# A float32 matmul in place of three split ones: the first expert's gate and up weights, and the first token tile's first projection

## The chip, the cores and the metric

One Trainium2 chip; the kernel uses one of its cores. The metric is the device time of one execution in microseconds (us), as the median of several executions. Engines are named as the profile names them: PE (TensorE matmuls; PEld its weight loads), DVE (VectorE), ACT (ScalarE), POOL (GpSimd), SP (SyncE, whose queue issues most loads).

## The reference, cut to what matters

Two layers over 512 tokens of 1024 features, all in float32: four attention mixers, then a mixture of 16 experts of which each token uses two.

```python
for layer in range(DEPTH):                       # 2
    h = rms_norm(x, norm1_g[layer])
    proj = jnp.einsum('bsd,dc->bsc', h, w_in[layer])
    ...
    x = x + jnp.einsum('bsm,md->bsd', mixed, w_out[layer])
    x = x + hier_moe(rms_norm(x, norm2_g[layer]), ...)

def hier_moe(h, wg, bg, we, be, w_gate, w_up, w_down):
    ...                                          # gate: top group, then top 2 experts of it
    for e in range(N_EXPERTS):                   # 16
        hid = jax.nn.silu(t @ w_gate[e]) * (t @ w_up[e])
        y = y + gate[:, e:e + 1].astype(t.dtype) * (hid @ w_down[e])
```

## The kernel before, in words

**Split operands.** Weights come in units of 128 x 1024 float32 (512 KB; the first projection's are 128 x 832). A unit is loaded into a buffer `raw`, and `split` (L142 to L145) makes of it two tiles in PE's rounded format: ACT copies `raw` to `hi`, and an engine E subtracts, `lo = raw - hi`; E is DVE, or POOL where the table `TAIL` says `sG`. Activations are split the same way (`hTh`/`hTl`, `xh`/`xl`, `hh`/`hl`). A product is then three matmuls, hi x hi, hi x lo, lo x hi (`mm3`, L263 to L269).

**The class `Weights`** keeps the units in order of use. A unit's `raw` is given back as soon as it is split, and the next load is issued on SP then; six units may be split ahead of PE (`HL = 6`).

**The start.** The 512 tokens are four tiles of 128. Tile t's rows are multiplied by the norm weights `g1` into `h` (`gained`, L587 to L593: tile 0 on DVE, tiles 1 to 3 on POOL in layer 0), turned by PE in eight pieces of 128 x 128 (`turned`), split, and multiplied with the first piece of `w_in`, 416 columns in four units (`proj`, L600). The rows' own scale `r0` is a chain of twelve small DVE operations (`rstd`, L124 to L135) and is put on by ACT when the product leaves PSUM (`ca`, L707); the sums of squares for it are ACT's `sq` (L585). ACT's order there is `ca` of tile 0, `sq` of tile 2, `hTh` of tile 2.

**Around the start of the experts.** The attention stage ends with a list of words in `TAIL`, which a small interpreter runs in that order: `x3` gathers expert 0's rows by matmul into `acc` (L1142), and then word list 69, "T K m sG B O q sG S": T turns `acc` into expert 0's `xh` and `xl`, K works out the gates on DVE (L1341 to L1368) and their three bf16 parts (L1334, L1336), m clears a buffer, sG splits a unit with POOL, B stores the last tile, O is a branch for overfull experts, q copies the token numbers, S issues the gather of expert 1's rows on POOL's DMA queue.

Then the loop over `MOE_ORDER` runs: gate and up of expert 0, then for each expert the next gate, this one's down, the next up. Each step splits what is ahead, multiplies one unit (`gu`, L1416; six matmuls of 512 columns) and frees it. Between expert 0's up units PE also runs the row lists `pli` (L1389, four small matmuls each), which need one-hot tiles `oh` from DVE (L341) and K's parts, and the eight transposes `ptg` of expert 1's rows (L1413).

Of the kernel before, what the change touches and what calls it, by code (L numbers as in the profile page):

```python
# [11 lines left out]
FT = mybir.dt.float32  # L12
# [3 lines left out]
AF = mybir.ActivationFunctionType  # L16
OP = mybir.AluOpType
AX = mybir.AxisListType

S = 512  # L20
D = 1024
NT = 4
# [3 lines left out]
CAP = 96  # L26
# [18 lines left out]
        66: "e1 sG c2",  # L45
        67: "f0 b3G o2 p0 r1V f1 h1 d2 o3 r2G e2 x0 p1 c3 d3 f2 e3 h30 x1 r3G p2 h2 f3",
        68: "x2 h31 p3 l x3",
        69: "T K m sG B O q sG S"}
WAITP = 5
JOIN = 52  # L50
STORES = ((13, 0, 1), (6, 1, 2), (1, 2, 3), (0, 3, 4))
# [11 lines left out]
def hybrid_encoder(ctx: ExitStack, tc: tile.TileContext, I: dict, out: bass.AP, depth=2, dbg=None):  # L63
# [10 lines left out]
    x_sb = cst.tile([128, NT, D], FT, name="x_sb")  # L74
# [68 lines left out]
    def split(hi, lo, src, E=V):  # L143
        A.activation(hi, src, AF.Copy)  # L144
        E.tensor_tensor(lo, src, hi.bitcast(FT), op=OP.subtract)  # L145

    class Weights:
# [4 lines left out]
        def __init__(self):  # L152
            self.spec, self.raw, self.hl, self.where = [], {}, {}, {}
            self.loaded = self.done = self.used = 0
            self.moe_pools = []
            self.held, self.paused = 0, False
            self.spare, self.spare_upto = [], 0

        def add(self, src, k, n, moe=False):
            self.spec.append((src, k, n, moe))  # L160
# [2 lines left out]
        def load(self, upto, q=SP, spare=False):  # L163
            while self.loaded < min(upto, len(self.spec)) and not self.paused:
# [22 lines left out]
                self.raw[u] = r  # L187
                self.loaded += 1

        def split(self, upto, E=V):  # L190

            while self.done < min(upto, self.loaded) and self.done < self.used + self.HL - self.held:
                u = self.done
                src, k, n, moe = self.spec[u]
                hi = wp.tile([128, 1024], FR, name="hi", bufs=self.HL)[:, :k * n]
                lo = wp.tile([128, 1024], FR, name="lo", bufs=self.HL)[:, :k * n]
                split(hi, lo, self.raw.pop(u), E)
                r = self.where.pop(u)
                if isinstance(r, bass.AP):
                    self.spare.append(r)  # L200
                self.hl[u] = (hi.rearrange("p (k n) -> p k n", k=k), lo.rearrange("p (k n) -> p k n", k=k))
                self.done += 1
                self.load(len(self.spec))
# [10 lines left out]
        def free(self, upto):  # L214
            for u in range(self.used, upto):
                del self.hl[u]
            self.used = upto

    W = Weights()
# [3 lines left out]
    def add_piece(key, w, c0, n, kc, per, moe=False, parts=1, pairs=False):  # L223

        if pairs:
            wv = w.rearrange("(i p j) n -> p i j n", p=128, j=2)
            us = [W.add(wv[:, k0 // 2:(k0 + per) // 2, :, c:c + n], per, n, moe)
                  for c in range(c0, c0 + parts * n, n) for k0 in range(0, kc, per)]
            wbase[key] = (us, per, n)
            return  # L230
        wv = w.rearrange("(k p) n -> p k n", p=128)
        us = [W.add(wv[:, k0:k0 + per, c:c + n], per, n, moe)
              for c in range(c0, c0 + parts * n, n) for k0 in range(0, kc, per)]
        wbase[key] = (us, per, n)
# [8 lines left out]
    for l in range(depth):  # L243
        wi = I['w_in'][l]
        for c0, n in ((0, 416), (416, 512), (928, 256)):
            add_piece((l, 'in', c0), wi, c0, n, 8, 4 if n == 256 else 2)
        add_piece((l, 'uq'), I['mla_w_uq'][l], 0, 384, 2, 2)
        add_piece((l, 'ukv'), I['mla_w_ukv'][l], 0, 512, 1, 1)
        for c0, n in ((1184, 512), (1696, 512), (2208, 256)):
            add_piece((l, 'in', c0), wi, c0, n, 8, 4 if n == 256 else 2)  # L250
        for m0, m1 in ((0, 2), (2, 3), (3, 4)):
            for n in range(2):
                add_piece((l, 'out', m0, n), I['w_out'][l][m0 * 256:m1 * 256], n * 512, 512, 2 * (m1 - m0), 2)
        for e, m in MOE_ORDER:
            src = {'g': 'expert_w_gate', 'u': 'expert_w_up', 'd': 'expert_w_down'}[m]
            if m == 'd':
                add_piece((l, e, m), I[src][l, e], 0, D, 4, 1, moe=True)
            elif (e, m) == (NE - 1, 'u'):

                add_piece((l, e, m), I[src][l, e], 0, FF // 2, 8, 4, moe=True, parts=2, pairs=True)  # L260
            else:
                add_piece((l, e, m), I[src][l, e], 0, FF, 8, 2, moe=True, pairs=True)

    def mm3(pt, lhs, ws, first=True, last=True):
        n, tot = 0, 3 * len(ws)
        for (lh, ll), (wh, wl) in zip(lhs, ws):
            for a, b in ((lh, wh), (lh, wl), (ll, wh)):
                PE.matmul(pt, a, b, start=first and n == 0, stop=last and n == tot - 1)  # L268
                n += 1  # L269
# [53 lines left out]
    for layer in range(depth):  # L323
# [32 lines left out]
        with ExitStack() as c2:  # L356
# [203 lines left out]
            with ExitStack() as c3:  # L560
# [26 lines left out]
                def gained(t):  # L587
                    hs[t] = hp.tile([128, D], FT, name="h", bufs=2)
                    for sl in finish_x(t) if finish_x else ():
                        if t == 0:  # L590
                            V.tensor_tensor(hs[t][:, sl], x_sb[:, t, sl], g1[:, sl], op=OP.mult)
                    if t > 0 or not finish_x:
                        (G if t else V).tensor_tensor(hs[t], x_sb[:, t], g1, op=OP.mult)  # L593

                def turned(t):
                    for k in range(0, 8, 4):
                        pt = turn([hs[t][:, (k + j) * 128:(k + j + 1) * 128] for j in range(4)])
                        split(hTh[t][:, k:k + 4], hTl[t][:, k:k + 4], pt.rearrange("p (a b) -> p a b", b=128))

                def proj(c0, t, evac):  # L600
                    us, per, n = wbase[layer, 'in', c0]
# [120 lines left out]

                ev_a = copy_to(ca[:, :, :416])
                for t in range(NT):
                    if t == 0:
                        gained(0)
                        warm(WARM[9] if layer else 0)
                        turned(0)
                        gained(1)
                        W.split(W.done + 2)  # L730
                        square(0)
                        W.split(W.done + 2)
                        r0 = rstd(sm, ss[:, 0:1], 1, 1.0 / D, "r0")
                        rs[0] = r0
                    else:
                        square(t)
                    if t == 1:
                        ev = proj(0, 0, ev_a)
                        turned(1)
                        ev()  # L740
                    if 0 < t < NT - 1:
                        gained(t + 1)
                    if t == 2:
                        ev = proj(0, 1, ev_a)
                        turned(2)
                    if t == 3:
                        r1 = rstd(sm, ss[:, 1:4], 3, 1.0 / D, "r1")
                        for j in range(3):
                            rs[j + 1] = r1[:, j:j + 1]
                        ev()  # L750
                        ev = proj(0, 2, ev_a)
                        turned(3)
                        W.split(W.done + 1)
                        ev()
# [33 lines left out]
            with ExitStack() as c3:  # L788
# [356 lines left out]
                def list_rows():  # L1145

                    pl = ps.tile([128, 512], FT, name="pli", tag="tr")
                    for t in range(NT):
# [4 lines left out]
                    X[1] = bass.IndirectOffsetOnAxis(ap=ix[:CAP], axis=0)  # L1153

                STAGES = dict(l=list_rows, b=norm_pair, c=turn_pair, o=open_out, d=close_out, e=turn_x, r=norm_x, f=logits, h=normed,
                              p=route, x=pick, s=lambda E: W.split(W.done + 1, E), w=warm)

                def tail(words):
                    for w in words.split():
# [148 lines left out]
        with ExitStack() as c2:  # L1308
# [69 lines left out]
            class Expert:  # L1378
# [24 lines left out]

                def turn(self, turned=None):
                    self.xh = sm.tile([128, 8, CAP], FR, name="xh", bufs=2)
                    self.xl = sm.tile([128, 8, CAP], FR, name="xl", bufs=2)
                    for k in range(0, 8, 4):
                        if turned:
                            pt = turned[k // 4]
                        else:  # L1410
                            pt = ps.tile([128, 4, CAP], FT, name="ptg", tag="tr")
                            for j in range(4):
                                PE.transpose(pt[:, j], self.g[:CAP, (k + j) * 128:(k + j + 1) * 128], ident[:CAP, :CAP])  # L1413
                        split(self.xh[:, k:k + 4], self.xl[:, k:k + 4], pt)

                def gu(self, m, i, w):  # L1416

                    if i == 0:
                        pool, tag = (pq, "pv") if m == 'u' else (ps, "mm") if self is not X[0] else (pq, "sc")
                        p = pool.tile([128, FF], FT, name="p" + m, tag=tag)  # L1420
                        setattr(self, 'p' + m, p[:CAP])
                    mm3(getattr(self, 'p' + m), [(self.xh[:, k], self.xl[:, k]) for k in (2 * i, 2 * i + 1)],
                        [(w[0][:, j], w[1][:, j]) for j in range(2)], first=i == 0, last=i == 3)

# [255 lines left out]
```

## Time and profile before

| | |
|---|---|
| median of 3 executions | 1385.62 us (1385.28 to 1387.55) |
| the profiled execution, its own time | 1387.39 us |
| its span, first to last instruction | 1385.6 us |
| mean granted TensorE clock | 0.969 of full |
| busy: PE, DVE, ACT, POOL | 1293.8, 1087.5, 876.4, 358.5 us |
| matmuls, DVE operations, ACT operations | 7222, 2108, 1439 |

The span has two layers of the same build. Layer 0's experts run from 386.8 to about 690 us, layer 1's from 1062.6 us to the end. The profiled execution's own time stands 1.8 us over its span and 1.8 us over the median.

### The profile page before, as it was taken

The page shows a single profiled execution, that of the slowest core. Times are in us where ns is not written, and L with a number is a line of the kernel's source. Part 1 is how long each engine was busy: PE and PEld are TensorE (multiplying, and loading weights), DVE is VectorE, ACT ScalarE, POOL GpSimd, SP SyncE. Part 2 cuts the span into 40 slices and gives each one's busy share as a digit, 9 for nine tenths or more (in the row PEclk, how much of TensorE's full clock was granted, in tenths as well). Part 3 has the DMA queues.
Part 4 walks back from the last instruction along what each step waited for, and adds up shares of the span by engine and source line. Part 5 has one row for each costly group of instructions (what it writes and reads, how often), then busy time and mean ns, then how long its engine had stood idle before and what let it go on. Part 6 is the DMA issues. An engine that isn't in the chain of part 4 may idle for free.

```text
span 1385.6 us, 21247 instructions
## 1 busy us (share of the span) xinstructions
PE 1293.8 (93%) x7222; PEld 1013.9 (73%) x7222; DVE 1087.5 (78%) x2108; ACT 876.4 (63%) x1439; POOL 358.5 (26%) x582
## 2 busy tenths in 40 slices
PE   8998899999969999999989998999998899999996
PEld 6776688888836666766777886888886566667674
DVE  4636776878688999999876488687876799999994
ACT  3443357766357888888744454676644588888884
POOL 4204324323422111111041152431345021111120
PEclk8999999999979999999999999999997899999999
DMA  7332251012699999999454223200176899999960
GB/s 198 116 97 62 83 177 51 18 60 108 257 334 292 370 363 373 359 361 332 124 136 123 91 77 79 69 28 28 62 296 222 292 351 368 370 363 366 367 206 13
DMA packets 100575, 278.46 MB, mean 201 GB/s; under 512 B 19465, under 2 KB 30521, under 8 KB 100456
## 3 DMA queue, kind: packets, MB, share of 16 engines
q1 hardware_dynamic: 89528, 247.95, 50.4%
q0 software_dynamic: 10352, 27.41, 7.9%
q10 hardware_dynamic: 576, 1.64, 0.4%
q8 instruction: 59, 0.97, 0.3%
q14 instruction: 60, 0.49, 0.1%
HBM read 264.34 MB, written 24.81 MB: 209 GB/s over the span
## 4 chain that ended last, share of the span: by engine, by line
PE 25%; DVE 17%; DMA 12%; issue 11%; ACT 4%; POOL 1%; POOLq 0%; DVEq 0%; ACTq 0%; SPq 0%
PE pm L268 9%; DVE lo L145 7%; PE pd L268 5%; DMA raw<-in_expert_w_down_dram 4%; DMA raw<-in_expert_w_gate_dram 3%; PE ptr L276 2%; DMA raw<-in_expert_w_up_dram 2%; PE pv L911 2%; PE pu L268 2%; ACT hi L144 2%; PE pg L268 2%; DMA out_dram<-ye,ix 1%; DVE oh L341 1%; ACT ye L1462 1%; DVE xl L145 1%
## 5 line engine op out<-in xcount | busy, mean ns | idle before, releaser
L145 DVE TENSOR_TENSOR lo<-raw,hi 128x1024 fp32r<-128x1024 f32 (+2 forms) x400 | 483.6, 1230 | 68.1 <-ACT hi L144 58.3
L144 ACT ACTIVATE hi<-raw 128x1024 fp32r<-128x1024 f32 (+1 forms) x410 | 422.7, 1050 | 92.6 <-PE pu L268 20.2
L268 PE MATMUL pm<-lo,hTh 128*128 128x512 f32 (+2 forms) x384 | 137.3, 358 | 6.8 <-DVE lo L145 5.1
L268 PE MATMUL pm<-hi,hTh 128*128 128x512 f32 (+2 forms) x384 | 139.3, 363 | 3.0 <-ACT hi L144 1.5
L268 PE MATMUL pm<-hi,hTl 128*128 128x512 f32 (+2 forms) x384 | 136.9, 356 | 0.4
L268 PE MATMUL pg<-lo,xh 128*96 128x512 f32 x256 | 104.0, 406 | 5.5 <-POOL lo L145 4.0
L268 PE MATMUL pu<-hi,xh 128*96 128x512 f32 (+1 forms) x272 | 109.0, 401 | 0.0
L268 PE MATMUL pg<-hi,xh 128*96 128x512 f32 x256 | 106.2, 415 | 2.4 <-ACTq L1478 1.4
L268 PE MATMUL pd<-hi,hl 128*96 128x512 f32 x256 | 102.1, 399 | 4.5 <-DVE hl L145 4.5
L268 PE MATMUL pu<-lo,xh 128*96 128x512 f32 (+1 forms) x272 | 105.7, 388 | 0.0
L268 PE MATMUL pu<-hi,xl 128*96 128x512 f32 (+1 forms) x272 | 104.8, 385 | 0.0
L911 PE MATMUL pv<-v,pT 128*128 128x64 f32 x768 | 98.3, 271 | 6.5 <-DVE pT L899 2.7
L268 PE MATMUL pg<-hi,xl 128*96 128x512 f32 x256 | 102.9, 402 | 0.6 <-DVE E L1349 0.6
L268 PE MATMUL pd<-lo,hh 128*96 128x512 f32 x256 | 101.2, 395 | 1.6 <-DVE lo L145 1.6
L882 ACT ACTIVATE p<-p,m 128x512 f32<-128x512 f32 x96 | 68.7, 716 | 52.2 <-DVE m L864 51.9
L911 PEld LDWEIGHTS pv<-v,pT 128*128 128x128 f32 x768 | 93.5, 192 | 10.8 <-DVE pT L899 4.8
L268 PE MATMUL pd<-hi,hh 128*96 128x512 f32 x256 | 100.7, 394 | 0.0
L268 PEld LDWEIGHTS pm<-lo,hTh 128*128 128x128 f32 x384 | 73.5, 191 | 18.2 <-DVE lo L145 9.8
L268 PEld LDWEIGHTS pm<-hi,hTh 128*128 128x128 f32 x384 | 73.8, 192 | 15.4 <-ACT hTh L144 2.4
L268 PEld LDWEIGHTS pm<-hi,hTl 128*128 128x128 f32 x384 | 73.5, 192 | 11.2 <-DVE hTl L145 2.1
L276 PE MATMUL ptr<-ident,p 128*128 128x128 f32 x512 | 76.9, 272 | 0.3
L276 PEld LDWEIGHTS ptr<-ident,p 128*128 128x128 f32 x512 | 63.3, 140 | 17.8 <-DVE pT L899 1.2
(371 smaller groups left out, 2746.6 us busy)
## 6 DMA issues: line engine op xcount, KB each, us to landing
raw<-in_expert_w_down_dram SPq DMA_DIRECT2D x116, 512.0 KB
raw<-in_expert_w_gate_dram SPq DMA_DIRECT2D x114, 512.0 KB
raw<-in_expert_w_up_dram SPq DMA_DIRECT2D x112, 512.0 KB
raw<-in_w_in_dram SPq DMA_DIRECT2D x32, 512.0 KB
raw<-in_w_out_dram SPq DMA_DIRECT2D x16, 512.0 KB
toep<-brep SPq DMA_DIRECT2D x16, 448.0 KB
x_sb<-in_expert_w_gate_dram SPq DMA_DIRECT2D x14, 512.0 KB
x_sb<-in_expert_w_down_dram SPq DMA_DIRECT2D x12, 512.0 KB
```

The lines of the kernel that those rows point to most:

```text
L144: A.activation(hi, src, AF.Copy)
L145: E.tensor_tensor(lo, src, hi.bitcast(FT), op=OP.subtract)
L268: PE.matmul(pt, a, b, start=first and n == 0, stop=last and n == tot - 1)
L276: PE.transpose(pt[:c, i * 128:(i + 1) * 128], s, ident)
L341: V.tensor_scalar(oh[:, t], iota, pos[:, t, e:e + 1], None, op0=OP.is_equal)
L882: A.activation(p, p, AF.Exp, bias=m, scale=-1.0, accum_out=s)
L911: PE.matmul(st['pv'][:, t], self.pT[:, k * 128:(k + 1) * 128], self.v(k), start=k == 0, stop=k == NT - 1)
L1462: A.activation(ye[:CAP, n * 512:(n + 1) * 512], self.pd[n], AF.Copy, scale=self.w)
```

## The change

In layer 0, tile 0's first projection piece is computed with plain float32 matmuls: PE reads `raw` itself and an unsplit, turned `hT`; one matmul stands for three. The four units are still split (tiles 1 to 3 need them), and tile 0's `hTh`/`hTl` are made from `hT` later, by ACT and POOL. The norm weights go onto tiles 1 and 2 on DVE, onto tile 3 on POOL.

In both layers expert 0's gate and up units, eight in all, are never split: PE reads `raw` and an unsplit `xh`, with one matmul for three, and a `raw` is given back when PE has used it. Word list 69 becomes "m S T B sV sV sV sV sV sV K O q": expert 1's gather comes first, and the units after the eight whole ones (expert 1's gate, expert 0's down) are split by DVE, ahead of K. The split of list 66, which took expert 0's first unit, now takes expert 1's first.

```diff
-        69: "T K m sG B O q sG S"}
+        69: "m S T B sV sV sV sV sV sV K O q"}
...
+        def room_for(self):
+            return sum(u not in self.whole for u in range(self.used, self.done)) < self.HL - self.held
+
+        def next(self):
+
+            while self.done in self.whole and self.done < self.loaded:
+                src, k, n, moe = self.spec[self.done]
+                self.hl[self.done] = self.raw.pop(self.done).rearrange("p (k n) -> p k n", k=k)
+                self.done += 1
+            return self.done
...
         def free(self, upto):
             for u in range(self.used, upto):
                 del self.hl[u]
+                if u in self.whole:
+                    self.leave(u)
+                    self.load(len(self.spec))
             self.used = upto
...
+                if e == 0:
+                    W.whole.update(wbase[l, e, m][0])
...
-                        (G if t else V).tensor_tensor(hs[t], x_sb[:, t], g1, op=OP.mult)
+                        (G if t > (0 if finish_x else 2) else V).tensor_tensor(hs[t], x_sb[:, t], g1, op=OP.mult)
...
+                def turned_whole():
+
+                    hT = oc[0].rearrange("p t c -> p (t c)")[:, :D].rearrange("p (k c) -> p k c", k=8)
+                    for k, copy in ((0, lambda o, i: A.activation(o, i, AF.Copy)), (4, V.tensor_copy)):
+                        pt = turn([hs[0][:, (k + j) * 128:(k + j + 1) * 128] for j in range(4)])
+                        copy(hT[:, k:k + 4], pt.rearrange("p (a b) -> p a b", b=128))
+                    return hT
...
+                    if t == 0 and layer == 0:
+                        gained(0)
+                        hT = turned_whole()
+                        gained(1)
+                        pm = ps.tile([128, 512], FT, name="pm", tag="mm")[:, :416]
+                        ev = lambda pm=pm: ev_a(0, pm)
+                        for i in range(3):
+                            proj_whole(hT, pm, i)
+                            W.split(W.done + 1)
+                            if i == 1:
+                                turned(1)
+                        square(0)
+                        gained(2)
+                        proj_whole(hT, pm, 3)
+                        W.split(W.done + 1)
+                        split(hTh[0], hTl[0], hT, G)
+                        r0 = rstd(sm, ss[:, 0:1], 1, 1.0 / D, "r0")
+                        rs[0] = r0
...
+                    if turned:
+
+                        self.xh = self.xh.bitcast(FT)
+                        A.activation(self.xh[:, :4], turned[0], AF.Copy)
+                        V.tensor_copy(self.xh[:, 4:], turned[1])
+                        return
...
+                    if self is X[0]:
+                        for j in range(2):
+                            k = 2 * i + j
+                            PE.matmul(getattr(self, 'p' + m), self.xh[:, k], w[:, j], start=k == 0, stop=k == 7)
+                        return
```

How the order moves at three places. First DVE and POOL at the start of layer 0, before (`h` is a tile times its norm weights, `lo` a weight unit's low part, `hTl` a turned tile's, `r0` tile 0's scale):

```order
L593 TENSOR_TENSOR h<-x_sb,g_112 128x1024
L145 TENSOR_TENSOR hTl_117<-ptr,hTh_113 128x512 x2
L145 TENSOR_TENSOR lo<-raw,hi 128x832 x4
L128 TENSOR_SCALAR r0v<-ss_133 128x1
L593 TENSOR_TENSOR h<-x_sb,g_112 128x1024 x3
```

The last row is POOL's, the others are DVE's. Now, DVE's first and POOL's two at the end:

```order
L613 TENSOR_TENSOR h<-x_sb,g_112 128x1024
L625 COPY qk_99<-ptr 128x512
L145 TENSOR_TENSOR lo<-raw,hi 128x832 x2
L145 TENSOR_TENSOR hTl_118<-ptr,hTh_114 128x512 x2
L145 TENSOR_TENSOR lo<-raw,hi 128x832
L128 TENSOR_SCALAR r0v<-ss_133 128x1
L145 TENSOR_TENSOR hTl_117<-qk_99,hTh_113 128x1024
L613 TENSOR_TENSOR h<-x_sb,g_112 128x1024
```

Between the rows shown DVE has two more `h`, one after the COPY and one ahead of the last `lo`. POOL's three `h` became one, behind a new operation on tile 0 that stands where DVE's `r0` chain runs.

Second, DVE at the start of the experts, before (`mxg` opens K, `oh` are the one-hot tiles, `row` reads a list):

```order
L145 TENSOR_TENSOR xl<-acc,xh 128x384 x2
L1341 TENSOR_REDUCE mxg<-lg 128x4
L1478 UNCONDITIONAL_BRANCH
L145 TENSOR_TENSOR lo<-raw,hi 128x1024 x5
L341 TENSOR_SCALAR oh<-iota,pos 128x96 x4
L145 TENSOR_TENSOR lo<-raw,hi 128x1024 x2
L1392 TENSOR_REDUCE row<-pli 96x1
```

And now:

```order
L1464 COPY xh<-acc 128x384
L145 TENSOR_TENSOR lo<-raw,hi 128x1024 x5
L1395 TENSOR_REDUCE mxg<-lg 128x4
L1540 UNCONDITIONAL_BRANCH
L361 TENSOR_SCALAR oh<-iota,pos 128x96 x8
L1446 TENSOR_REDUCE row<-pli 96x1
```

Five splits moved ahead of K, the seven between K and the first `row` are gone, and so are the four that stood among the lists.

Third, PE in the same place, now (before, each matmul with `raw` was three, with hi, lo and hi):

```order
L1482 MATMUL pg<-raw,xh 96x512 x8
L1482 MATMUL pu<-raw,xh 96x512 x2
L1443 LDWEIGHTS oh
L1443 MATMUL pli<-parts,oh 96x5
L1470 MATMUL ptg<-ident,xg 128x96 x8
```

The places of the lists and of the transposes among the up units are as before.

## Rows read from the trace of the kernel before

**Rows 1.** By stretch: PE, PEld, DVE, ACT, POOL busy; PE clock, DMA share, GB/s.
```profile
440.00:480.00 40.00, 39.62 (x195) 27.82 (x194) 37.40 (x50) 32.69 (x41) 9.92 (x5) 1.00 1.02 366
...
404.00:412.00 8.00, 4.72 (x19) 3.43 (x20) 5.93 (x20) 0.35 (x1) 0.98 (x1) 0.63 0.98 392
```

**Rows 2.** Timeline, PE, steady experts: start, duration, engine, line.
```profile
499.91 0.39 PE L268 MATMUL pd<-hi,hh 128*96 128x512 f32 x1
...
500.14 0.40 PE L268 MATMUL pd<-lo,hh 128*96 128x512 f32 x1
```

**Rows 3.** Waits of PE, 386 to 420 us: total, times, longest.
```profile
PE pli L1389 <- DVE oh L341: 6.8, 3, 3.3
```

**Rows 4.** Timeline, start of layer 0's experts.
```profile
386.78 0.71 PE L268 MATMUL pg<-hi,xh 128*96 128x512 f32 x1 [0.84 <-PEq L1478]
...
386.98 0.16 DVE L1341 TENSOR_REDUCE mxg<-lg 128x4 f32<-128x16 f32 x1
...
390.62 2.38 DVE L1336 TENSOR_TENSOR first<-gate,parts 128x64 f32<-128x64 f32 x1
...
393.03 3.17 DVE L1334 CAST parts<-first 128x64 bf16<-128x64 f32 x1
...
397.96 5.77 DVE L145 TENSOR_TENSOR lo<-raw,hi 128x1024 fp32r<-128x1024 f32 x5 [1.14 <-DVEq L1478]
...
407.67 0.80 DVE L341 TENSOR_SCALAR oh<-iota,pos 128x96 bf16<-128x96 f32 x4
...
408.62 0.72 PE L268 MATMUL pu<-hi,xh 128*96 128x512 f32 x1
...
411.28 1.48 PE L1413 MATMUL ptg<-ident,xg 96*128 96x96 f32 x8
...
414.13 0.31 PE L1389 MATMUL pli<-parts,oh 128*96 128x5 bf16 x4
...
416.68 0.72 PE L268 MATMUL pu<-hi,xh 128*96 128x512 f32 x1
...
419.34 0.59 PE L268 MATMUL pg<-hi,xh 128*96 128x512 f32 x1
```

**Rows 5.** Timeline, layer 1: first gate matmul of expert 0, and of expert 1.
```profile
1062.62 0.71 PE L268 MATMUL pg<-hi,xh 128*96 128x512 f32 x1
...
1094.13 0.63 PE L268 MATMUL pg<-hi,xh 128*96 128x512 f32 x1
```

**Rows 6.** By line: count, duration in ns (least, median, most), of PE's small matmuls.
```profile
L115 PE MATMUL pb<-oh,rb x32: 212/214/218, 51.2 to 149.1; 32*8 32x64 f32 x32
...
L1115 PE MATMUL pp<-M,tri x20: 169/169/183, 359.6 to 1056.7; 128*128 128x16 bf16 x20
...
L911 PE MATMUL pv<-v,pT x768: 222/275/323, 211.3 to 1029.7; 128*128 128x64 f32 x192
```

**Rows 7.** By line, 9 to 20 us and the whole span: DVE's splits, a scale's step.
```profile
L145 DVE TENSOR_TENSOR lo<-raw,hi x4: 1012/2114/3209, 10.1 to 17.3; 128x832 fp32r<-128x832 f32 x4
...
L134 DVE TENSOR_TENSOR r0f<-r0f,r0y x6: 158/159/163, 19.0 to 712.5; 128x1 f32<-128x1 f32 x6
```

**Rows 8.** Timeline, start of layer 0: POOL, ACT and PE.
```profile
10.19 6.32 POOL L593 TENSOR_TENSOR h<-x_sb,g 128x1024 f32<-128x1024 f32 x2 [9.72 <-DMA x_sb<-in_x_dram]
...
22.13 2.39 POOL L593 TENSOR_TENSOR h<-x_sb,g 128x1024 f32<-128x1024 f32 x1 [5.62 <-PE ptr L276]
...
22.57 0.61 ACT L707 ACTIVATE ca<-pm,r0y 128x416 f32<-128x416 f32 x1
23.05 1.07 ACT L585 ACTIVATE sq<-x_sb 128x1024 bf16<-128x1024 f32 x1
...
28.52 0.45 PE L268 MATMUL pm<-hi,hTh 128*128 128x416 f32 x1 [0.25 <-ACT hTh L144]
```

**Rows 9.** Busy time by stretch: the last experts of layer 0, and of layer 1.
```profile
660.00:680.00 20.00, 20.00 (x99) 14.29 (x98) 18.35 (x19) 16.72 (x21) 1.44 (x1) 1.00 0.53 168
...
1340.00:1360.00 20.00, 20.00 (x96) 14.25 (x95) 18.37 (x19) 16.78 (x21) 1.44 (x1) 1.00 0.07 11
```

More of the change, by code (lines that the diff above doesn't have):

```diff
@@ L157, in __init__ @@
             self.spare, self.spare_upto = [], 0
+            self.whole = set()
         def add(self, src, k, n, moe=False):
@@ L188, in load, with leave @@
                 self.loaded += 1
+        def room_for(self):
[6 more added lines that the diff above has]
+            return self.done
+        def leave(self, u):
+            r = self.where.pop(u)
+            if isinstance(r, bass.AP):
+                self.spare.append(r)
         def split(self, upto, E=V):
-            while self.done < min(upto, self.loaded) and self.done < self.used + self.HL - self.held:
+            while self.next() < min(upto, self.loaded) and self.room_for():
                 u = self.done
@@ L197, in split @@
                 split(hi, lo, self.raw.pop(u), E)
-                r = self.where.pop(u)
-                if isinstance(r, bass.AP):
-                    self.spare.append(r)
+                self.leave(u)
                 self.hl[u] = (hi.rearrange("p (k n) -> p k n", k=k), lo.rearrange("p (k n) -> p k n", k=k))
@@ L216, in free @@
                 del self.hl[u]
+                if u in self.whole:
+                    self.leave(u)
+                    self.load(len(self.spec))
             self.used = upto
@@ L598, in turned, with proj_whole @@
                         split(hTh[t][:, k:k + 4], hTl[t][:, k:k + 4], pt.rearrange("p (a b) -> p a b", b=128))
+                def turned_whole():
[4 more added lines that the diff above has]
+                    return hT
+                def proj_whole(hT, pm, i):
+                    src, k, n, moe = W.spec[i]
+                    w = W.raw[i].rearrange("p (k n) -> p k n", k=k)
+                    for j in range(k):
+                        PE.matmul(pm, hT[:, i * k + j], w[:, j], start=i + j == 0, stop=i * k + j == 7)
                 def proj(c0, t, evac):
@@ L724, in hybrid_encoder @@
                 for t in range(NT):
-                    if t == 0:
+                    if t == 0 and layer == 0:
[16 more added lines that the diff above has]
+                        rs[0] = r0
+                    elif t == 0:
                         gained(0)
@@ L737, in hybrid_encoder @@
                     if t == 1:
-                        ev = proj(0, 0, ev_a)
-                        turned(1)
+                        if layer:
+                            ev = proj(0, 0, ev_a)
+                            turned(1)
                         ev()
-                    if 0 < t < NT - 1:
+                    if (1 if layer == 0 else 0) < t < NT - 1:
                         gained(t + 1)
@@ L1155, in hybrid_encoder @@
                 STAGES = dict(l=list_rows, b=norm_pair, c=turn_pair, o=open_out, d=close_out, e=turn_x, r=norm_x, f=logits, h=normed,
-                              p=route, x=pick, s=lambda E: W.split(W.done + 1, E), w=warm)
+                              p=route, x=pick, s=lambda E: W.split(W.next() + 1, E), w=warm)
                 def tail(words):
@@ L1405, in turn @@
                     self.xh = sm.tile([128, 8, CAP], FR, name="xh", bufs=2)
+                    if turned:
[3 more added lines that the diff above has]
+                        return
                     self.xl = sm.tile([128, 8, CAP], FR, name="xl", bufs=2)
                     for k in range(0, 8, 4):
[L1408 to L1413, printed above, removed]
+                        pt = ps.tile([128, 4, CAP], FT, name="ptg", tag="tr")
+                        for j in range(4):
+                            PE.transpose(pt[:, j], self.g[:CAP, (k + j) * 128:(k + j + 1) * 128], ident[:CAP, :CAP])
                         split(self.xh[:, k:k + 4], self.xl[:, k:k + 4], pt)
```

## The prediction

> **What bounds the kernel now.** I first read the table of busy time by stretch. In steady experts PE is busy 39.62 of 40 us at full granted clock [rows 1]; the timeline shows its 512-column rounded matmuls 0.231 us apart (500.14 − 499.91) [rows 2]. There PE bounds, and what the change saves on ACT, DVE and POOL buys nothing. The DMA share is 1.02 beside it, so DMA is close behind. At the start of the experts it is different: in 404 to 412 us PE is busy 4.72 of 8 us and the granted clock is 0.63 [rows 1]. The list of waits tells for what: three times, 6.8 us in all, for DVE's one-hot tiles `oh` [rows 3].
>
> The timeline of that start then gives the two spans that the change can shorten. In layer 0, expert 0's gate and up run from 386.78 to 419.34, where expert 1's gate begins [rows 4]: 32.6 us. In layer 1 they run from 1062.62 to 1094.13 [rows 5]: 31.5 us. Their 48 matmuls at 0.231 us would be 11.1 us, so about two thirds is waiting and low clock. Who makes PE wait is DVE: the gates' work K starts at 386.98, and two of its operations on 64 elements a partition take 2.38 and 3.17 us where K's first takes 0.16 [rows 4]; POOL is splitting units then. After K come five splits (5.77 us), and only at 407.67 the first `oh` [rows 4].
>
> **The price of a float32 matmul.** No row shows one of 512 columns. The nearest are three small ones; each is recorded as two passes. From 16 to 64 columns a pass goes from 169 to 214 ns [rows 6], so (214 − 169)/48 = 0.94 ns a column; a 512-column pass is 0.48 us, a matmul 0.96 us at full clock and 1.92 at half. One 16-column row is bf16, so this is an estimate. Low bound: a pass at the rounded spacing [rows 2], 0.46 for the two. High bound: another 64-column pass takes 275 ns [rows 6]; (275 − 169)/48 = 2.2 ns a column counts fixed cost as columns, and 1.7 ns, which is (275 − 169)/64, still does; I take 1.7 us a matmul, 3.4 at half clock. I use 0.96, since both rows of its slope lie closest in price to a stream of columns. The three rounded matmuls that it replaces are 0.69 us. In work alone the change is thus a loss for PE, of 0.27 x 16 = 4.3 us a layer; it can only pay by taking waits away.
>
> **The experts' start, after.** DVE is free for the next word at 386.98, as before. Now five splits come first, 5.8 us [rows 4], to 392.8. K and the branch took 397.96 − 386.98 = 11.0 us, of which 2.38 + 3.17 − 2 x 0.16 = 5.2 was the stretching of two operations; POOL has no split there now, so 5.8, to 398.6. Eight `oh` at 0.80/4 are 1.6 us, the reading of the first list some 0.45, and from an `oh` to PE's next up matmul it is 408.62 − 407.67 = 0.95 [rows 4]. PE resumes at 401.6, 14.8 us after its first gate matmul. Its ten float32 matmuls ahead of that (eight gate, two up), two at half clock and eight at full, take 3.8 + 7.7 = 11.5 us, to 398.3; so DVE's list, and not the dearer matmul, sets this point, with 3.3 us to spare.
>
> Behind it PE has six float32 matmuls, the eight transposes (1.48 us [rows 4] at the clock granted there, some 1.0 at full) and the rest of the lists, which cost 416.68 − 414.13 = 2.55 [rows 4], less 0.80 for four `oh` that are ready earlier: 1.75. At full clock 6 x 0.96 + 1.0 + 1.75 = 8.5, at half 6 x 1.92 + 1.48 + 1.75 = 14.8. PE will have stood idle for some 3 us just before, and a granted clock of 0.63 was seen where it was busy 4.72 of 8 us [rows 1]; I take the middle, 11.6. Expert 1's gate then begins 26.4 us after expert 0's: in layer 0 6.2 us sooner, in layer 1 5.1 us. **11.3 us gained**, between 4.9 and 17.5 by the clock alone (23.3 or 29.6 us in place of 26.4).
>
> What of that lasts? The loads must keep up with experts that come sooner. In 1340 to 1360 us PE is busy 20.00 of 20 while the DMA share is 0.07 [rows 9]: the last weights landed 20 us and more before use, so 5 us more demand is covered. In layer 0 the share is already 0.53 in 660 to 680 [rows 9]. The gather of expert 1's rows, issued earlier in the list, still waits for the stored rows to land and was not late before; I cost it at nothing. Without that cover its wait would show ahead of the transposes. Eight splits a layer leave ACT, DVE and POOL; none of these is on the path in the experts. The late return of a `raw` buffer costs nothing as long as the above holds, since a whole unit takes a `raw` but none of the six split places.
>
> **The start of layer 0, after.** Before, the next thing that PE needs after tile 0's piece is `hTh` of tile 2, at 28.52, which stands on ACT behind `ca` of tile 0, 22.57 to 23.18, and `sq` [rows 8]; `ca` needs `r0`. Now h(1) goes to DVE, about 1.25 us (a split of 832 columns that nothing holds takes 1.01 [rows 7], times 1024/832), and h(2) too. POOL's two operations of 3.16 us from 10.19 [rows 8] are gone, which had stretched DVE's splits to 3.21 [rows 7]. But the fourth unit's load is issued behind the first split, which comes 1.25 later, so the last split still ends near 17 to 18 us. Then POOL does tile 0's low part and h(3), each 128 x 1024 like the row of 2.39 [rows 8]: 18.1 to 22.9. Just there DVE runs the twelve steps of `r0`, 0.16 each [rows 7] and 2.2 with their gaps. If they are held as K's two operations were, `r0` is ready at 25.1; `ca` 0.61, `sq` 1.07 [rows 8] with some 0.2 between, and half of a tile's `hTh` 0.55 follow, and PE begins tile 2 at 27.5: 1.0 sooner. It will have been idle for some 5 us; the 24 matmuls of 416 columns behind it take 24 x 0.188 = 4.5 us at full clock, 3.8 more if half that lasted a little short of their end. From +1.0 to −2.8; I take the middle: **1.0 lost**.
>
> That POOL holds r0's steps is a choice. The row for it is K's (128 x 64, stretched to 2.38 and 3.17 [rows 4]); no row shows 128 x 1 beside POOL, so the other end is no hold at all, which is the first rival. The Trainium skill, "SBUF: State Buffer", section "SBUF: two separate sides", says that DVE and GpSimd share a pair of ports under a lock that is held for the whole instruction, with the loser blocked; by that rule the two-input steps of `r0` are held and the start is worth −1.0, without it +4. The stretched rows agree with it, for large and 64-column operations.
>
> **Sum.** 11.3 − 1.0 = 10.3. The profiled execution's span is 1385.6, so 1375.3; its own time of 1387.39 would be 1377.1. The runs' median, 1385.62, is 1.8 below that execution's own time, so the median comes out at 1375.3 too.
>
> **Rivals.**
>
> (1) *POOL does not hold r0.* Then `ca` runs near 20.7 instead of 25.1, tile 2 begins by 23.5, and the start gains about 4 (3.4 to 5.2). For: steps of 0.16 us may slip between. Against: K's stretched rows. 1385.6 − 11.3 − 4.0 = 1370.3.
>
> (2) *Half clock through every float32 stretch.* The experts gain only 4.9, the start loses 2.8: 1383.5, no change that can be told. For: clock 0.63 in this very stretch. Against: it was low because PE waited, and float32 keeps it busier.
>
> (3) *DMA paces the experts*, at a share of 1.02 [rows 1]: what PE gains it waits for later, 11.3 is given back, and the start's 1.0 lost: 1386.6. Against: PE's busy 20.00 of 20 with DMA at 0.07 [rows 9].
>
> (4) *A float32 pass costs one column a cycle* (0.46 a matmul): the tail is 5.5 at full and 8.8 at half clock, mean 7.1, so 4.5 more a layer: 1366.3.
>
> (5) *The float32 matmul is dear*, the rival on the other side. Place: expert 0's sixteen matmuls a layer. They and the 3.0 us of lists and transposes fit into the 32.6 and 31.5 us of before only up to (31.5 − 3.0)/16, about 1.8 us for a mean matmul; from there PE's own work sets the point where expert 1 begins, and the change loses. With the high bound, a mean of 1.7 and 3.4 or 2.55 us, the stretch is 16 x 2.55 + 3.0 = 43.8: 11.2 and 12.3 lost, and the start's 2.8: about 1412. For: the 275 ns rows [rows 6]. Against: much of those 275 ns is likely fixed.
>
> **How the numbers follow.** The forecast has 0.50, with a range of its own of 1368 to 1382 (the clock ends of both layers are unlikely to fall together). Rivals: (1) 0.18, (2) 0.12, (3) 0.05, (4) 0.06, (5) 0.09. 1366 to 1384 takes in the forecast, (1), (2) and the edge of (4), and leaves out (3), (5) and the forecast's tails, not over 0.2. A difference of 0.2% is 2.8 us, about what a measurement of this kernel can tell from no change. Faster by more: forecast, (1) and (4), 0.74. Within it: (2) and (3), 0.17. Slower: (5), 0.09.
>
> **What would show it.** In the profile of the changed kernel: two records for each `pg<-raw` matmul, near 0.48 us apart at full clock; the step from the second up unit to the third about 14.8 us after the first gate matmul, and PE waiting for `oh` ahead of it; expert 1's gate 26.4 us after expert 0's in both layers; K's two operations short again; steady experts with 0.231 us a matmul and PE as busy as before. In the start: POOL from about 18 to 23 us, `r0`'s last step near 25 (forecast) or 20.5 (rival 1), tile 2's first matmul near 27.5 or 23.5. I am wrong if PE reaches the lists later than DVE has them, if passes are more than 0.8 us apart, or if PE waits for loads in later experts.

## The result, and the profile after

The changed kernel takes 1396.43 us (median of 8 runs, 1393.06 to 1404.43) against 1388.22 for the kernel before (8 runs, 1385.28 to 1390.85). The ratio is 1.0069, 95% interval 1.0047 to 1.0092: **slower by 0.7%**, some 9.6 us, where 10.3 us of gain had been forecast. The profiled execution took 1400.43 us, its span is 1398.6 us, the mean granted clock 0.967. PE is busy 1300.7 us, DVE 1063.7, ACT 857.4, POOL 345.4.

Where the time went is seen when the same matmuls are laid side by side (PE's timeline, start in us):

| PE's matmul | before | after | difference |
|---|---|---|---|
| tile 2's first projection | 28.52 | 26.21 | −2.3 |
| layer 0, last `pv` ahead of the first `x_sb` sums | 343.46 | 346.08 | +2.6 |
| layer 0, `ptr<-ident,x_sb` behind them | 347.66 | 355.89 | **+8.2** |
| layer 0, expert 1's first gate matmul | 419.34 | 423.80 | +4.5 |
| layer 0, last `py` | 712.56 | 720.06 | +7.5 |
| layer 1, `ptr<-ident,x_sb` | 1022.53 | 1037.30 | **+14.8** |
| layer 1, expert 1's first gate matmul | 1094.13 | 1106.69 | +12.6 |
| end of the span | 1385.6 | 1398.6 | +13.0 |

From expert 0's first gate matmul to expert 1's, PE gained 6.5 us in layer 0 and 1.1 in layer 1, but the end of the attention stage lost 5.6 and 7.4 us (8.2 − 2.6, and 14.8 from 7.4 at the last `pv` there), at a place of which the forecast had no term. A further 2.6 us went in layer 0 between the `x_sb` transposes and expert 0's gate (41.8 us, 39.1 before); PE's waits there are as before, and the mean granted clock is 0.91 from 355 to 397 us against 0.98 from 347 to 387 before. The timeline of the changed kernel where the sums into `x_sb` are made, PE, ACT and DVE, then SP:

```profile
346.93 0.28 PE L296 MATMUL ptr<-ident,y 128*128 128x128 f32 x1
351.44 0.50 PE L288 MATMUL pm<-hi,mh 128*128 128x512 f32 x1 [4.24 <-DVE x_sb L1103]
...
348.47 1.06 ACT L144 ACTIVATE hi<-raw 128x1024 fp32r<-128x1024 f32 x1 [7.92 <-DMA raw<-in_expert_w_gate_dram]
...
349.56 1.23 DVE L145 TENSOR_TENSOR lo<-raw,hi 128x1024 fp32r<-128x1024 f32 x1 [6.72 <-ACT hi L144]
350.71 1.28 DVE L1103 TENSOR_TENSOR x_sb<-x_sb,pm 128x512 f32<-128x512 f32 x2
...
341.48 2.17 SPq L187 DMA_DIRECT2D raw<-in_expert_w_gate_dram  x4
```

Read it from below. SP issues expert 1's gate loads at 341.48. ACT, whose next word is to split the first of them, waits 7.92 us for it, to 348.47. DVE waits 6.72 us for ACT's high part, and only then adds the projection to `x_sb`. PE waits 4.24 us for that sum. Then it runs at a lower clock, as this table of busy time shows (PE, PEld, DVE, ACT, POOL, clock, DMA, GB/s):

```profile
340.00:350.00 10.00, 6.99 (x36) 5.36 (x34) 3.14 (x10) 1.61 (x3) 3.53 (x14) 1.00 0.93 360
350.00:356.00 6.00, 4.56 (x13) 3.56 (x14) 5.37 (x21) 2.31 (x9) 1.35 (x7) 0.72 1.03 410
```

In layer 1 the same chain stands, with 8.83 us on ACT, 7.63 on DVE and 5.15 on PE. In the kernel before ACT began the corresponding split at 337.82 without any wait (its timeline, ACT, then SP):

```profile
337.82 1.07 ACT L144 ACTIVATE hi<-raw 128x1024 fp32r<-128x1024 f32 x1
...
198.56 0.33 SPq L186 DMA_DIRECT2D raw<-in_expert_w_gate_dram  x1
```

This is the split word of **list 64** ("sV d0", on DVE), two lists ahead of the one that the text on the change names; list 66's word finds no free place in either kernel. Before, it took expert 0's first unit, whose load had been issued at 198.56, 139 us earlier in layer 0. Now expert 0's eight units are whole and are passed over, and it takes the ninth unit in the order of loading, which SP issued only after ACT had come to the word (348.47 − 7.92 = 340.55).

The experts' start, answering to [rows 4, 5]: PE, ACT and DVE in layer 0, then PE and ACT in layer 1. A float32 matmul stands there as two passes, so that x16 are eight matmuls.

```profile
397.66 8.09 PE L1482 MATMUL pg<-raw,xh 128*96 128x512 f32 x16 [0.30 <-DMA raw<-in_expert_w_down_dram]
409.67 3.44 PE L1482 MATMUL pu<-raw,xh 128*96 128x512 f32 x4 [3.92 <-DVEq L1540]
414.64 1.94 PE L1482 MATMUL pu<-raw,xh 128*96 128x512 f32 x4
421.71 0.74 PE L1443 MATMUL pli<-parts,oh 128*96 128x3 bf16 x4 [2.61 <-DVE oh L361]
423.80 1.42 PE L288 MATMUL pg<-hi,xh 128*96 128x512 f32 x1
...
417.85 1.28 ACT L1489 ACT_TABLE_LOAD   x1 [12.25 <-SPq L1540]
...
420.14 1.02 DVE L145 TENSOR_TENSOR xl<-ptg,xh 128x384 fp32r<-128x384 f32 x2 [4.92 <-ACT xh L144]
...
1076.29 8.40 PE L1482 MATMUL pg<-raw,xh 128*96 128x512 f32 x16 [0.37 <-PEq L1540]
1103.34 0.78 PE L1443 MATMUL pli<-parts,oh 128*96 128x3 bf16 x4 [4.96 <-DVE oh L361]
1106.69 1.42 PE L288 MATMUL pg<-hi,xh 128*96 128x512 f32 x1
...
1099.47 1.28 ACT L1489 ACT_TABLE_LOAD   x1 [15.31 <-SPq L1540]
```

From expert 0's first gate matmul to expert 1's it is 26.1 us in layer 0 (32.6 before) and 30.4 in layer 1 (31.5 before); to the first down matmul `pd` behind that it is 33.9 (38.6 before) and 38.1 (38.1 before), so that layer 1 keeps nothing. A second chain is to be seen: ACT's silu, behind the branch, waits 12.25 and 15.31 us for SP; `xh` of expert 1 stands behind silu, DVE's `xl` behind that, the last one-hot tiles behind `xl`, and PE waits 2.61 and 4.96 us for them. In the kernel before the same wait on ACT was 1.88 and 1.69 us. The program says what SP does there: the end of the branch on SP waits for all eight of its load queues, so for every load that SP issued ahead of the branch; and five splits now stand ahead of it, each of which gives back a `raw` and so issues a load. The trace has these waits, eight in each layer, the first passed at 406.8 us, with 10.1 us of standing between them in layer 0 (the change, the instructions of L1540; then SP's waits from 380 to 420 us: total, times, longest):

```profile
L1540 SPq EVENT_SEMAPHORE  x16: 17/17/17, 406.8 to 1099.4; - x16
...
SPq L1540 <- SPq L1540: 10.1, 7, 2.5
```

### The profile page after: what moved, and what is told of

Same layout as the page of the kernel before. It is cut to its first block, busy times and chain, and to the rows that moved or that the text cites. A ratio compares the mean times of both kernels' runs of the same rounds, so it can differ in the third digit from the quotient of the medians.

```text
span 1398.6 us, 21090 instructions
## 1 busy us (share of the span) xinstructions
PE 1300.7 (93%) x7182; PEld 1011.1 (72%) x7182; DVE 1063.7 (76%) x2095; ACT 857.4 (61%) x1419; POOL 345.4 (25%) x577
## 5 line engine op out<-in xcount | busy, mean ns | idle before, releaser
L145 DVE TENSOR_TENSOR lo<-raw,hi 128x1024 fp32r<-128x1024 f32 (+1 forms) x388 | 464.7, 1219 | 80.9 <-ACT hi L144 71.9
L144 ACT ACTIVATE hi<-raw 128x1024 fp32r<-128x1024 f32 (+1 forms) x394 | 406.3, 1050 | 112.0 <-PE pg L288 25.8
L288 PE MATMUL pm<-lo,hTh 128*128 128x512 f32 (+2 forms) x376 | 133.2, 354 | 5.1 <-DVE lo L145 5.1
L288 PE MATMUL pm<-hi,hTl 128*128 128x512 f32 (+2 forms) x376 | 133.5, 355 | 0.3
L288 PE MATMUL pu<-hi,xh 128*96 128x512 f32 (+1 forms) x256 | 100.1, 391 | 0.0
L288 PE MATMUL pg<-hi,xh 128*96 128x512 f32 x240 | 98.7, 411 | 0.0
L288 PE MATMUL pu<-lo,xh 128*96 128x512 f32 (+1 forms) x256 | 97.3, 380 | 0.0
L288 PE MATMUL pu<-hi,xl 128*96 128x512 f32 (+1 forms) x256 | 96.5, 377 | 0.0
L288 PE MATMUL pg<-lo,xh 128*96 128x512 f32 x240 | 95.6, 398 | 0.0
L288 PE MATMUL pg<-hi,xl 128*96 128x512 f32 x240 | 94.6, 394 | 0.0
L288 PEld LDWEIGHTS pm<-lo,hTh 128*128 128x128 f32 x376 | 71.6, 190 | 14.9 <-DVE lo L145 6.5
```

## The experiments

Each kernel was timed beside the kernel before on the same chip, with 5 to 12 executions; the ratio is to that kernel, with its 95% interval. Different runs were on different chips, so they are compared by their ratios. The last columns are the us from expert 0's first gate matmul to expert 1's, by layer, in the profiled execution. They are single values: e4's experts are those of the kernel before and e6's those of e5, and the columns differ by up to 2.6 us.

| run | ratio (interval) | layer 0 | layer 1 |
|---|---|---|---|
| kernel before | 1 | 32.6 | 31.5 |
| the change | 1.0069 (1.0047 to 1.0092) | 26.1 | 30.4 |
| e1: list 64 without its split | 0.9952 (0.9935 to 0.9970) | 27.7 | 26.9 |
| e2: e1 and the splits behind the branch | 0.9878 (0.9859 to 0.9896) | 24.5 | 24.8 |
| e3: e1 and K ahead of the splits | 0.9958 (0.9941 to 0.9975) | 30.2 | 29.2 |
| e4: the start of layer 0 alone | 0.9977 (0.9963 to 0.9991) | 30.0 | 31.1 |
| e5: e2 without early splits | 0.9941 (0.9923 to 0.9959) | 29.0 | 28.5 |
| e6: e5, start as before | 0.9953 (0.9939 to 0.9967) | 27.9 | 28.5 |
| e7: kernel before, e5's order | 0.9952 (0.9937 to 0.9966) | 29.1 | 29.3 |
| e8: e2 with two early splits | 0.9882 (0.9857 to 0.9908) | 22.6 | 21.3 |
| e9: e2 with three early splits | **0.9850** (0.9831 to 0.9870) | 21.3 | 22.0 |
| e10: e2 with list 64's split | 0.9996 (0.9975 to 1.0017) | 24.1 | 24.7 |

**e1, list 64 without its split.**

```diff
-        64: "sV d0",
+        64: "d0",
```

> The changed kernel without the split word of list 64, so that expert 1's first gate unit is split by list 66, on POOL, some 8 us later. Theory A (the loss is that list 64's split now waits for a load issued only 7 us before: ACT stood 7.9 and 8.8 us for it, DVE behind ACT, PE 4.2 and 5.2 us behind DVE, then at low clock): both layers' steps at the output projection go, 6.7 + 7.3 us, so some 1396.4 - 14 = 1382, faster than the kernel before by 0.4%. Rival B (the loads are late in any case and whoever takes the unit first waits): the wait shows at list 66, on POOL and ACT, and the time stays within 3 us of 1396. Rival C (the float32 matmuls are what is slow): the wait goes, but less than 4 us of time with it.

Measured 1381.68 us, ratio 0.9952, as theory A had it. List 66's word takes the unit now. POOL splits it without a wait for the load, and PE's sums at the old place have none (e1's timeline, ACT, POOL, PE):

```profile
360.62 1.06 ACT L144 ACTIVATE hi<-raw 128x1024 fp32r<-128x1024 f32 x1
...
361.77 2.35 POOL L145 TENSOR_TENSOR lo<-raw,hi 128x1024 fp32r<-128x1024 f32 x1 [2.79 <-ACT hi L144]
...
351.13 0.28 PE L296 MATMUL ptr<-ident,y 128*128 128x128 f32 x1
351.17 0.48 PE L288 MATMUL pm<-hi,mh 128*128 128x512 f32 x1
```

Rivals B and C fall: the load, issued at 345.69 in this execution, is not late for a split that begins 14.9 us behind it, and float32 matmuls are not what was slow.

**e2, the splits behind the branch.** The counterpart of the second chain.

```diff
-        64: "sV d0",
+        64: "d0",
-        69: "m S T B sV sV sV sV sV sV K O q"}
+        69: "m S T B K O q sV sV sV sV sV sV"}
```

> As the first, and list 69 reads m S T B K O q and then the six splits, so that the loads which the splits free are issued behind the branch. Theory D (silu, the first ACT operation behind the branch, stands 12.2 and 15.3 us for the loads that the splits issued ahead of the branch; DVE's third one-hot tiles stand behind ACT's xh, PE behind them for 2.6 and 5.0 us): ACT's wait shrinks to a few us, PE's wait for the third list goes, 7.6 us less than the first run, some 1375. Rival E (silu stands for the stored rows or for PE's gate product, not for loads): ACT's wait and PE's third wait stay, and the time equals the first run's within 2 us.

Measured 1371.59 us, ratio 0.9878. Silu's wait shrinks from e1's 14.03 and 12.80 us to 2.47 (for DVE) and 3.02, and of PE's long waits one is left, for the first list (e2, timeline of ACT, layers 0 and 1, then PE's list of waits from 385 to 430 us: total, times, longest):

```profile
397.75 1.28 ACT L1489 ACT_TABLE_LOAD   x1 [2.47 <-DVE oh L361]
...
1067.40 1.28 ACT L1489 ACT_TABLE_LOAD   x1 [3.02 <-SPq L1540]
...
PE pli L1443 <- DVE oh L361: 5.3, 3, 3.6
PE pg L1482 <- PEq L1540: 0.5, 1, 0.5
```

**e3, K ahead of the splits, the branch behind them.**

```diff
-        64: "sV d0",
+        64: "d0",
-        69: "m S T B sV sV sV sV sV sV K O q"}
+        69: "m S T B K sV sV sV sV sV sV O q"}
```

> As the first, and list 69 reads m S T B K, then the six splits, then O q: K is ahead of the splits, but the branch is not. By theory D nothing changes: the loads are still ahead of the branch and DVE comes to the one-hot tiles at the same time, so the first run's time within 2 us, and ACT's wait of 12 to 15 us behind the branch stays. If the place of K by itself were what matters (rival F), this run would be as fast as the second.

Measured 1381.81 us, 0.9958, e1's time. Silu still waits 15.11 and 14.65 us for SP. The place of K by itself is worth nothing; what counts is whether the splits, with the loads that they free, stand ahead of the branch. PE's waits tell by which way (e3, 385 to 430 us: total, times, longest):

```profile
PE pli L1443 <- DVE oh L361: 4.9, 2, 4.2
PE pu L1482 <- DVEq L1540: 3.9, 1, 3.9
```

Ahead of the first list PE waits about as long for DVE in e3 (3.9 us, and 3.1 in layer 1) as in e2 (3.6 and 3.9). What goes is the wait for the third list, behind silu: 4.2 and 4.1 us in e3, 0.7 in both layers of e2. That is 6.9 of the 10 us between the two; the rest has no wait of its own, but the mean granted clock from the first gate matmul to expert 1's is 0.78 and 0.79 in e3, 0.86 in e2. In e1, with the same wait of silu, PE comes to the third list late itself, at a clock of 0.75 and 0.82, and waits only 0.9 and 2.5 us.

**e10, the square of the two edits.** List 64's split kept, the splits behind the branch.

```diff
-        69: "m S T B sV sV sV sV sV sV K O q"}
+        69: "m S T B K O q sV sV sV sV sV sV"}
```

> The changed kernel with list 64's split kept and only list 69 in the second run's order (m S T B K O q, then the splits). It completes a square of two edits. If the two losses are separate, this run keeps list 64's wait (ACT 8 us for the load, PE 4 to 5 us, both layers, some 14 us in all) and loses the waits behind the branch: the ratio to the changed kernel is that of the second run to the first, 0.993, so 1.0069 x 0.993 = 0.9995 to the kernel before. If the wait at list 64 were needed for the loss behind the branch, or hid it, the ratio would be near 1.007 or near 0.988.

Measured 0.9996. ACT's waits for the load are back (e10's timeline, ACT and then PE, layers 0 and 1):

```profile
346.05 1.06 ACT L144 ACTIVATE hi<-raw 128x1024 fp32r<-128x1024 f32 x1 [8.61 <-DMA raw<-in_expert_w_gate_dram]
...
1020.71 1.06 ACT L144 ACTIVATE hi<-raw 128x1024 fp32r<-128x1024 f32 x1 [8.68 <-DMA raw<-in_expert_w_gate_dram]
...
349.01 0.80 PE L288 MATMUL pm<-hi,mh 128*128 128x512 f32 x1 [4.94 <-DVE x_sb L1103]
...
1023.68 0.79 PE L288 MATMUL pm<-hi,mh 128*128 128x512 f32 x1 [5.00 <-DVE x_sb L1103]
```

The square: list 64's split costs 1.0069/0.9952, so 1.2%, or 0.9996/0.9878, 1.2% (16 us); the branch behind the splits costs 1.0069/0.9996, 0.7%, or 0.9952/0.9878, 0.7% (10 us). By the intervals each price is known to some 5 us. The two losses are separate and add.

**e4, the start of layer 0 alone**, experts as before.

```diff
-        69: "m S T B sV sV sV sV sV sV K O q"}
+        69: "T K m sG B O q sG S"}
...
-                if e == 0:
-                    W.whole.update(wbase[l, e, m][0])
```

> Only the start of layer 0 as in the change (tile 0 by float32 matmuls, h of tiles 1 and 2 on DVE); experts as before. Theory G (tile 2 begins 2.3 us sooner, but PE then waits for the row of the first relative bias at about 80 us, so nothing is left): the time of the kernel before within 1 us. The forecast's step said 1.0 lost. Rival H (the start's DVE and ACT order delays the attention stage, where the changed kernel was 1.6 to 2.4 us behind at 220 us): 2 to 3 us slower than before.

Measured 1385.57 us against 1389.24, 0.9977: some 3 us faster (1.3 to 5.1 by the interval), neither theory's number. Rival H falls. That more than theory G's 1 us is left was not expected, and single profiles do not show where: in e4's, tile 2 begins 2.3 us sooner, at 171 us it stands 2.8 us behind the profile of before, and at 1063 us still 0.4 behind.

**e5, no early splits.**

```diff
-        64: "sV d0",
+        64: "d0",
-        69: "m S T B sV sV sV sV sV sV K O q"}
+        69: "m S T B K O q"}
```

> As the second run, without the six split words in list 69 (m S T B K O q): the units behind the whole ones are split between the up units. Theory I (in the second run the five splits behind the branch, 5.8 us of DVE, are what PE still waits for at the first two lists, 3.6 us and 1.0 us in layer 0): PE reaches the up units 3 to 4 us sooner in each layer, some 6 us less than the second run, a ratio of about 0.983 to the kernel before. Rival J (the same splits then stand ahead of the third one-hot tiles and of expert 1's low part, and hold PE there): equal to the second run within 2 us.

Measured 0.9941, slower than e2 by 0.6%: a miss in the direction of rival J, and worse than it. The timeline (ACT, DVE, PE, layer 0):

```profile
400.32 1.28 ACT L1489 ACT_TABLE_LOAD   x1 [10.92 <-SPq L1540]
...
403.18 1.23 DVE L145 TENSOR_TENSOR lo<-raw,hi 128x1024 fp32r<-128x1024 f32 x1 [9.15 <-ACT hi L144]
...
405.67 0.78 PE L1443 MATMUL pli<-parts,oh 128*96 128x5 bf16 x4 [8.10 <-DVE oh L361]
```

Silu comes to its wait sooner, and the next high part stands behind silu on ACT. DVE's low part waits 9.15 us for it with the second list's one-hot tiles behind it, and PE 8.10 us. In e2 the high parts stand ahead of silu, so that its wait has nobody behind it. It is the same wait as in the change, reached from the other side.

**e6, e5 with the start as before** (the four edits of the start taken back, tile 0 by split operands).

> As the fifth run, with the start of layer 0 as in the kernel before (tile 0 by split operands, h of tiles 1 to 3 on POOL). By the run of the start alone (ratio 0.998) the start is worth some 3 us: this is 3 us slower than the fifth run. If the start's gain is lost at the waits of the attention stage it is equal to it within 1 us.

Measured 0.9953 against e5's 0.9941: 0.12%, 1.7 us, with intervals that overlap, so that this pair alone cannot be told from none. With e4, the start is worth some 2 to 3 us of gain.

**e7, the kernel before with e5's order**, all units split.

```diff
-        69: "T K m sG B O q sG S"}
+        69: "m S T B K O q"}
```

> The kernel before with one edit: list 69 reads m S T B K O q (gather first, no early splits), expert 0's gate and up split as before. It tells how much of the fifth run is the order of the words and how much the whole float32 units. Theory K (whole units are what lets PE run the gate and the lists without DVE): PE waits for the low parts of all seven gate and up units that are still to be split, 1.15 us of DVE each, between K and the lists, so a gain of no more than 2 to 3 us a layer against the kernel before, ratio 0.995 to 1.000. Rival L (the order alone does it, POOL no longer holding K): ratio 0.988 or below, as the second run.

Measured 0.9952, inside theory K's numbers: moving POOL's splits and the gather alone gives half a per cent. With the splits left to the expert loop, whole units (e6, 0.9953) gain nothing over it. With splits put behind the branch more is gained: e2 is 0.7% below e7, and e9 1.0%, the start's 0.1 to 0.2% included. The kernel before, its units all split, was not run with e2's or e9's order, so how much of that is owed to the whole units is not shown.

**e8 and e9, two or three early splits** behind the branch.

```diff
-        64: "sV d0",
+        64: "d0",
-        69: "m S T B sV sV sV sV sV sV K O q"}
+        69: "m S T B K O q sV sV"}
```

(e9: "m S T B K O q sV sV sV".)

> As the second run, with two of the six splits behind the branch (m S T B K O q sV sV); the others fall behind the second list and later. Theory M (in the second run DVE's five low parts, 5.8 us, are what PE waits for at the first list, 3.6 and 3.9 us; in the fifth run the loss was that ACT's first high part stood behind silu and DVE's one-hot tiles behind that): with two high parts ahead of silu and two low parts ahead of the one-hot tiles the first wait goes and no long one takes its place; 3 to 7 us less than the second run, a ratio of about 0.984. Rival N (silu's wait for the loads ahead of the branch holds a later split, and so the third list and expert 1's low part, as in the fifth run): ratio 0.990 or above.

> As the second run, with three of the six splits behind the branch. By theory M the first list's wait is shorter by 2 x 1.15 us than in the second run, and no split stands ahead of the third list: 2 to 4 us less than the second run, ratio about 0.986. By rival N 0.990 or above.

Measured 0.9882 and 0.9850: theory M for e9 (0.986 expected), not for e8. PE's list of waits at layer 0's experts, e8 and then e9:

```profile
PE pli L1443 <- DVE oh L361: 3.6, 2, 2.9
```

```profile
PE pli L1443 <- DVE oh L361: 1.7, 2, 1.0
```

With two, a later split's low part comes ahead of the third list's one-hot tiles (2.9 us); with three, none does. e9, at 1367.81 us where the kernel before took 1389.51, is the fastest version seen, 1.5% below the kernel before and some 2% below the change; e2, e8 and e9 have 5 or 6 executions each, and their intervals overlap.

## Why the prediction was wrong, point by point

**The sum left out one moved word.** The step that failed is "What of that lasts?", which asked of the loads only whether the last experts' come in time [rows 9] and found cover. The word of list 64 was never priced. A split that skips eight units takes the ninth, and the ninth's load was issued 7 us before the split could begin. Its price is 13 us in the two profiles (5.6 and 7.4, up to the `x_sb` transposes) and 16 us by e1 and e10; it alone turns the forecast's sign. None of the five rivals named it: the one on the slow side was the dear float32 matmul.

**"Behind it PE has ... the rest of the lists", 1.75 us.** This term was too small by the 2.6 and 5.0 us that PE waited for the third list. The forecast moved five splits ahead of K and the branch and priced their 5.8 us of DVE, but not the five loads that they issue on SP, which silu then waits for. e2 and e3 show it: 10 us by the square, of which PE's wait for the third list is the larger part. "The late return of a `raw` buffer costs nothing" stands untested; the early return of others is what cost.

**The float32 matmul**: forecast 0.96 us at full clock. Sixteen passes of e2's first gate in layer 1 take 1060.90 − 1053.99 = 6.91 us, so 0.43 a pass and 0.86 a matmul:

```profile
1053.99 7.08 PE L1482 MATMUL pg<-raw,xh 128*96 128x512 f32 x16 [0.30 <-PEq L1540]
1060.90 1.88 PE L1482 MATMUL pu<-raw,xh 128*96 128x512 f32 x4
```

The slope of two small rows was a tenth too high, and closer than either bound; rivals (4) and (5) fall. That it came so close is partly luck: its 16-column row `pp` is a bf16 matmul recorded once (20 matmuls in two layers, x20), not one of two passes as the forecast read it.

**The resumption, 14.8 us after the first gate matmul**, was 17.0 (414.64 − 397.66) and 15.6 us. K's operations were short again, as said, and DVE had its first one-hot tile at 409.42, 11.8 us after the gate, just as forecast. But PE waited 3.92 and 3.20 us for DVE to pass the branch, with one up unit (two matmuls) still to do behind that wait, which the forecast had put ahead of it.

**26.4 us from expert to expert** was 26.1 and 30.4. In layer 0 the number came out by luck, 17.0 + 9.2 us where 14.8 + 11.6 was forecast: PE resumed 2.2 us late, and the tail, the unpriced wait of 2.6 us included, was 2.4 shorter, at a clock of 0.98 from 414 to 424 us where the middle between full and half had been taken. In layer 1 the tail was 14.8 us, at 0.73 from 1092 to 1107 us, with 4.96 of waiting in it.

**The start**: the mechanism was right, the sign of its sum wrong. DVE's and POOL's timeline:

```profile
18.30 1.92 DVE L133 SCALAR_TENSOR_TENSOR r0f<-r0v,r0y 128x1 f32<-128x1 f32 x1
20.25 2.33 DVE L134 TENSOR_TENSOR r0f<-r0f,r0y 128x1 f32<-128x1 f32 x1
22.61 0.16 DVE L135 SCALAR_TENSOR_TENSOR r0y<-r0f,r0y 128x1 f32<-128x1 f32 x1
...
17.80 2.40 POOL L145 TENSOR_TENSOR hTl<-qk,hTh 128x1024 fp32r<-128x1024 f32 x1 [17.34 <-ACT hTh L144]
20.17 2.39 POOL L613 TENSOR_TENSOR h<-x_sb,g 128x1024 f32<-128x1024 f32 x1
```

POOL does hold `r0`: two of its steps take 1.92 and 2.33 us in place of 0.16, each to the end of one POOL operation, and rival (1) falls. The rule of the Trainium skill that was weighed there ("SBUF — State Buffer", section "SBUF: two separate sides") agrees with it, now with rows of one element a partition: the two steps have two inputs, and the one-input steps at 17.92 and 18.11 us, beside the same POOL operation, kept their 0.15 us. But `r0` was done at 23.9, not 25.1, and tile 2 began at 26.21, not 27.5: 2.3 us sooner. The clock then fell as feared (0.72 from 26 to 32 us, 1.00 before), and 0.8 us was left at the transposes behind tile 2's matmuls (32.76, 33.53 before). Measured by e4 and e6, the start gains 2 to 3 us where 1.0 lost had been taken from the middle of +1.0 and −2.8.

## What to carry to other kernels

When a table of words says "split the next unit" and a change makes units skip that step, every such word in the program takes another unit: list each of them, with the time at which its unit's load is issued and the engines that stand in order behind the wait. Price a moved split by the load that it frees as well as by its engine's time, above all ahead of a branch whose end waits for every load. That a dearer matmul (0.86 us for three of 0.23) pays by itself is not shown here: with no early splits, whole and split units came out equal (e6 and e7). Most of the gain hung on where the remaining splits were put: 1.0069 and 0.9850 are the same matmuls.

## What the runs showed of the hardware that was not expected

Single executions of the same program differ by several us through the granted clock in the attention stage. e1 and e2 are the same up to list 69, and their profiled executions come to expert 0's first gate matmul at 394.24 and 385.21 us, 9 us apart; the same matmuls stand 2.2 us apart at 196 us and 7.6 at 212. In e1's profiled execution (1391.91 us, where its median is 1381.68) the clock from 206 to 212 us is 0.50 with PE busy 6.00 of 6 us, behind a stretch in which PE was busy 4.78 of 6; in e2's profile the same stretch, with the same program up to there, is at 1.00 (both by stretch, e1 and then e2):

```profile
200.00:206.00 6.00, 4.78 (x25) 4.50 (x26) 1.20 (x3) 2.15 (x5) 1.78 (x3) 0.72 0.71 235
206.00:212.00 6.00, 6.00 (x27) 5.40 (x25) 2.73 (x5) 2.08 (x6) 0.72 (x1) 0.50 0.03 9
```

```profile
200.00:206.00 6.00, 6.00 (x49) 5.55 (x48) 3.75 (x9) 4.16 (x10) 0.73 (x1) 1.00 0.52 196
206.00:212.00 6.00, 6.00 (x51) 5.61 (x50) 3.98 (x11) 3.47 (x8) 1.65 (x2) 1.00 0.00 0
```

So a difference of a few us between two profiles is no evidence by itself, which is why the start's gain could not be placed; medians of several executions carry it. What starts the low stretch in one execution and not in another stays open.
